# Layer 0's last head in written order, with the first half of its output projection in pieces among it

## The chip, the cores and the metric

The kernel runs on one core of a Trainium2 chip. A core has a matrix engine (TensorE, PE in the profile; its weight loads are shown apart as PEld), three engines that work on elements (VectorE = DVE, ScalarE = ACT, GpSimd = POOL), and a queue that issues transfers (SyncE, SP). Each engine works through its own instructions in program order and waits on semaphores for what the others must have done. The metric is the device time of one execution in microseconds (us).

## What is computed

The program is a two-layer encoder over 1024 tokens of width 1024 in float32. Layer 0 mixes tokens by differential attention, layer 1 by latent attention, and each is followed by a gated MLP with a short convolution. The change lies in layer 0's attention, which is:

```python
def diff_attention(h, w_qkv, ..., subln_g, w_o, lambda_init, cos, sin):
    q, k, v = jnp.split(h @ w_qkv, 3, axis=-1)      # 8 heads; q, k: 2 x 64 wide, v: 128 wide
    q, k = rope on the first 16 of 64 columns
    def block(qb, blk):                              # blocks of 128 queries
        sc = einsum('bqhcd,bkhcd->bhcqk', qb, k) * scale
        p = masked_softmax(sc, chunk_mask(blk, s))
        a = p[:, :, 0] - lam * p[:, :, 1]
        return einsum('bhqk,bkhe->bqhe', a, v)
    o = from_blocks(lax.map(block, ...))
    o = rms_norm(o, subln_g) * (1.0 - lambda_init)
    return o.reshape(b, s, D_MODEL) @ w_o            # then x = x + this
```

The body above is shortened to what matters; the mask is causal by chunks of 64 tokens.

## The kernel before

**Products in three parts.** Operands of TensorE's products are split into a high part (a copy to the short format fp32r, by ACT at L127 or DVE) and a low part (the source less the high part, by DVE or POOL, L130). A product is the sum of three matmuls (L119, L120, L121): high by low, high by high, low by high. So a weight costs a cast (`b` below) and a subtraction (`c`) before it can be used.

**Layer 0's attention.** Eight heads, each in four steps p = 0..3 of two 128-query tiles; step number t = 4 x head + p, 0 to 31. A step scores its queries against the keys up to them (L1804/L1805, two components), takes maxima (DVE), exponentials (ACT, L1830), inverts the sums (DVE), scales the first component's probabilities (ACT L147, or POOL L149 for p < 2), subtracts the second component's (DVE, L1843), transposes them on TensorE against an identity (L1851), splits the transposes, and multiplies with the values. The sum is copied by ACT (L1879). After every second step the head's output (128 x 512 tokens) is normalised: two squares on ACT (L1885, L1888), the low part on POOL, a sum of squares on TensorE (a product with ones, L1896/L1897), roots on ACT, a step of Newton on DVE, and the result is stored in DRAM as o_d (L1917). Meanwhile the next head's keys, queries and values are made in units of half a product each (24 + 12 + 12 matmuls, in PSUM bank u, of which there is one), with rotary mixing (DVE swap and cosine L657, POOL L685), and the next head's weights are split.

**What sets the order.** The function `da_steps` issues the parts of all steps. For t < 28, heads 0 to 6, it reads a row of the table `DA_SCORE` (one of four rows, by t % 4), under a manual schedule, which keeps the engines to the written order. A token of a row is a part's name, with `'` for a step earlier and `+` for the next step: S scores, M maxima, E exponentials, I inverse, C scale, X mix, T transposes, H and L the high and low split of them, A product with the values, O copy, Q squares, F sum of squares, R roots, N Newton; U and V are the step's one or two projection units (`0` and `1` the half-products, `s` and `m` swap and cosine, `p` and `a` POOL's two rotary instructions, `k*` and `q*` the key and query splits, `c t h l` a value's copy, turn and split); Wh and Wl are the high and low part of the next head's weight (Wl on POOL). For t >= 28, head 7, the manual schedule is closed: the parts are issued in an order that depends only on `DA_WHOLE`, and the scheduler that places all the rest of the program places them by its own priorities, so that it may mix head 7 with what stands around it.

**What stands around it.** The output projection w_o comes in eight tiles of 128 rows, one for each head. `prefetcher` loads its tiles 0 to 3 (`step`, called in each of head 7's four `prepare` calls), splits them into the places s0 to s7 as those come free (tile 1's and 3's low part on DVE, the others' on POOL), and loads tiles 4 to 7 into u10 to u13 after head 7. Then `project_first` multiplies the outputs of heads 0 to 3 with w_o's tiles 0 to 3: for each of eight token tiles (in the order 0, 4, 1, 5, 2, 6, 3, 7) it loads the tile of o (L729) into a ring, splits it into two 512-wide pieces of s12, makes two products of 12 matmuls, and adds them to x (into bank u and in two additions for the first four, into one big bank S and in one for the others). After that `project_rest` does the same with the outputs of heads 4 to 7: its first token tile needs the o_d that the last steps of head 7 store.

Of the kernel before, what the change touches and what calls it, by code (L numbers as in the profile page):

```python
# [11 lines left out]
F32R = mybir.dt.float32r  # L12
# [44 lines left out]
class Trunk:  # L57
# [223 lines left out]
    def steps(self, attend, units, prepare, n, apart=False):  # L281
# [3 lines left out]
        for t in range(n + 2):  # L285
# [25 lines left out]
            if t >= 2:  # L311
# [11 lines left out]
    DA_WHOLE = ("S0 M0 M0a M0b E0a E0b I0 C0 X0 S1 M1 M1a M1b E1a E1b I1 C1 X1 Wh Wl "  # L323
                "T0 H0 L0 T1 H1 L1 T2 H2 L2 A0 T3 H3 L3 A1 A2 A3 O Q1 Q2 Q3 F R1 R2 R3 N1 N2 N3").split()

    def da_steps(self, attend, units, prepare, n):
# [3 lines left out]
        region = ExitStack()  # L330
        region.enter_context(self.tc.manual_schedule(engines={E.PE, E.DVE, E.Activation, E.Pool}))
        steps, last = [], 28
        for t in range(-1, n + 2):
            while len(steps) < min(n, t + 2 if t + 1 < last else t + 1):
                x = len(steps)
                steps.append(attend(x))
                steps[x].parts.update(prepare(x))
                us = units(x)
                if x < last:
                    for x, u in zip("UV", us):  # L340
                        steps[-1].parts.update({x + name: f for name, f in u.items()})
            if t >= n:
                us = []
            if t == last:
                region.close()
            if t == 99:
                region.enter_context(self.tc.high_priority())
            for name in self.DA_SCORE[t % 4].split():
                step = t - name.count("'") + name.count("+")
                if 0 <= step < min(n, last):  # L350
                    steps[step](name.strip("+'"))
            if t < last:
                continue
            now = steps[t] if t < n else None
            old = steps[t - 1] if t > last and t <= n else None
            older = steps[t - 2] if t - 2 >= last else None
            if now:
                now("Wh", "Wl", "S0", "M0", "M0a", "M0b", "E0a", "E0b")
            for u in us:
                u.pop("0")()  # L360
            if old:
                old(*self.DA_WHOLE[: self.DA_WHOLE.index("A1")])
            if now:
                now("I0", "C0", "X0", "S1", "M1", "M1a", "M1b", "E1a", "E1b")
# [1891 lines left out]
```

## Time and profile before

| what | us |
|---|---|
| median of three runs (lowest, highest) | 2424.54 (2423.31, 2424.95) |
| the profiled execution | 2427.72 |
| its span (first to last instruction) | 2425.9 |

The profiled execution is one of its own, and about 3 us longer than the median. Its TensorE clock was granted at 0.993 of full speed in the mean.

How to read the rows below: `L1851` is line 1851 of the kernel printed above. `b<-ident,u` says that an instruction writes a tile b and reads tiles ident and u, with numbers left out: tiles u, s and h are places in SBUF of 128 x 1024, 128 x 2048 and 128 x 512 elements, tiles b and S banks in PSUM (and the projection products' bank is also called u). In a timeline a row has start, length, engine, line and operation, shapes, how many instructions were put together, and in brackets how long the engine had been idle before and what ended that. The stretch in question runs from 423.6 us (head 7's first step) to about 540 us (the second half of the output projection); steps of head 0 lie from about 45 us.

### The profile page before, as it was taken

What the parts mean: (1) busy time and instruction counts of PE and PEld (TensorE: products, weight loads), DVE (VectorE), ACT (ScalarE), POOL (GpSimd) and SP (SyncE); (2) the same over time, 40 slices, a digit from 0 to 9 for tenths busy, and PEclk for the clock granted to TensorE, in tenths of its full rate; (3) what the DMA queues carried; (4) which work ended last, traced back from release to release, by engine and by line L of the source; (5) the groups of instructions that cost most, each with busy time, mean ns of one, the idle gap of its engine ahead of it and who ended that gap; (6) DMA issues with size and microseconds to landing.
All of it is one profiled execution on the core that took longest, in us unless ns stands there. A gap on an engine that the chain in (4) does not pass through costs nothing.

```text
span 2425.9 us, 32597 instructions
## 1 busy us (share of the span) xinstructions
PE 2355.7 (97%) x11936; PEld 1999.6 (82%) x11936; DVE 1960.6 (81%) x3175; ACT 1290.5 (53%) x2366; POOL 623.5 (26%) x489
## 2 busy tenths in 40 slices
PE   7999999989999999999999999999989999999998
PEld 7888888778888888878899789988878888887886
DVE  6888888847888888899964788887488888888997
ACT  5677767645444444444445777776344444444444
POOL 4555555424100000000041666664330000000001
PEclk9999999999999999999999999999999999999999
DMA  4011111332222222553221210124322222227502
GB/s 153 31 44 36 35 49 53 105 92 98 94 83 79 87 79 87 189 178 128 76 100 46 77 40 29 49 62 135 92 87 87 78 88 86 79 87 277 172 2 78
DMA packets 95792, 213.91 MB, mean 88 GB/s; under 512 B 8720, under 2 KB 33936, under 8 KB 95632
## 3 DMA queue, kind: packets, MB, share of 16 engines
q1 hardware_dynamic: 86448, 184.04, 23.3%
q10 hardware_dynamic: 9184, 27.79, 3.1%
q8 instruction: 94, 1.54, 0.3%
q14 instruction: 66, 0.54, 0.1%
HBM read 159.37 MB, written 52.43 MB: 87 GB/s over the span
## 4 chain that ended last, share of the span: by engine, by line
PE 82%; DVE 7%; DMA 4%; ACT 3%; POOL 2%; issue 2%; SPq 0%; POOLq 0%; DVEq 0%; ACTq 0%
PE S L119 13%; PE S L121 13%; PE S L120 13%; PE b L119 8%; PE b L120 8%; PE b L121 8%; PE u L119 3%; PE u L121 3%; PE u L120 3%; PE b L252 2%; DVE s L130 2%; PE u L1961 1%; PE u L1960 1%; PE S L1804 1%; PE S L1805 1%
## 5 line engine op out<-in xcount | busy, mean ns | idle before, releaser
L167 POOL TENSOR_TENSOR st<-st,mhalf 128x1 f32<-128x1 f32 x56 | 37.2, 665 | 1308.7 <-DVE st L164 1300.2
L119 PE MATMUL S<-s,u 128*128 128x512 f32 (+1 forms) x768 | 290.3, 378 | 9.4 <-DVE s L130 3.9
L127 ACT CAST u<-h 128x512 fp32r<-128x512 f32 (+2 forms) x242 | 145.8, 619 | 280.9 <-DVE h L988 279.8
L121 PE MATMUL S<-s,u 128*128 128x512 f32 (+1 forms) x768 | 289.3, 377 | 0.1
L120 PE MATMUL S<-s,u 128*128 128x512 f32 (+1 forms) x768 | 289.1, 376 | 0.0
L119 PE MATMUL b<-s,u 128*128 128x512 f32 x588 | 230.8, 392 | 1.8 <-DVE u L130 1.3
L121 PE MATMUL b<-s,u 128*128 128x512 f32 x588 | 229.0, 390 | 0.0
L120 PE MATMUL b<-s,u 128*128 128x512 f32 x588 | 229.0, 389 | 0.0
L1045 DVE SCALAR_TENSOR_TENSOR u<-u,conv,u 128x1023 f32<-128x1023 f32 (+1 forms) x176 | 226.0, 1284 | 1.4 <-ACT u L1041 1.4
L149 POOL TENSOR_TENSOR u<-u,st 128x384 f32<-128x384 f32 (+7 forms) x160 | 172.1, 1084 | 174.8 <-DVE st L1946 104.9
L127 ACT CAST s<-u 128x512 fp32r<-128x512 f32 (+3 forms) x230 | 144.9, 665 | 112.3 <-PE u L121 35.5
L119 PE MATMUL u<-s,s 128*128 128x512 f32 (+1 forms) x440 | 177.2, 403 | 4.0 <-DVE h L657 2.8
L119 PEld LDWEIGHTS S<-s,u 128*128 128x128 f32 x768 | 145.1, 189 | 37.4 <-DVE s L130 4.5
L120 PE MATMUL u<-s,s 128*128 128x512 f32 (+1 forms) x440 | 172.4, 392 | 0.0
L121 PE MATMUL u<-s,s 128*128 128x512 f32 (+1 forms) x440 | 172.4, 392 | 0.0
L130 DVE TENSOR_TENSOR u<-b,u 128x512 fp32r<-128x512 f32 (+1 forms) x256 | 158.7, 631 | 15.5 <-ACT u L127 13.1
L127 ACT CAST u<-b 128x512 fp32r<-128x512 f32 (+1 forms) x256 | 134.7, 546 | 68.6 <-PE b L1851 36.3
L121 PEld LDWEIGHTS S<-s,u 128*128 128x128 f32 x768 | 145.0, 189 | 26.7 <-DVE u L130 0.5
L120 PEld LDWEIGHTS S<-s,u 128*128 128x128 f32 x768 | 145.1, 189 | 26.2
L130 DVE TENSOR_TENSOR s<-u,s 128x512 fp32r<-128x512 f32 (+2 forms) x210 | 151.1, 753 | 14.5 <-ACT s L127 14.1
L1048 ACT ACTIVATE u<-u 128x1024 f32<-128x1024 f32 x44 | 46.7, 1062 | 187.8 <-DVE u L1045 187.7
L130 DVE TENSOR_TENSOR u<-h,u 128x512 fp32r<-128x512 f32 x164 | 112.7, 687 | 32.9 <-ACT u L127 31.8
(280 smaller groups left out, 6570.1 us busy)
## 6 DMA issues: line engine op xcount, KB each, us to landing
u<-in_ffn_up SPq DMA_DIRECT2D x88, 512.0 KB, 4.1
g_d<-u ACTq DMA_DIRECT2D x44, 512.0 KB, 2.6
u<-in_ffn_down SPq DMA_DIRECT2D x66, 256.0 KB, 4.6
u<-g_d SPq DMA_DIRECT2D x62, 256.0 KB, 4.2
s<-in_da_wqkv SPq DMA_DIRECT2D x23, 512.0 KB, 3.6
x_d<-u SPq DMA_DIRECT2D x16, 512.0 KB, 2.9
s<-x_d SPq DMA_DIRECT2D x8, 1024.0 KB, 11.3
u<-o_d SPq DMA_DIRECT2D x24, 256.0 KB, 3.1
```

Of the source, the lines that this page charges most:

```text
L119: mm(out, lh, rl, start=first, stop=False, skip_group_check=onto)
L120: mm(out, lh, rh, start=False, stop=False, skip_group_check=onto)
L121: mm(out, ll, rh, start=False, stop=last, skip_group_check=onto)
L127: self.nc.scalar.copy(out, src)
L130: (eng or self.nc.vector).tensor_sub(out, src, hi.bitcast(F32))
L149: self.nc.gpsimd.tensor_mul(x, x, s.to_broadcast(list(x.shape)))
L167: nc.gpsimd.tensor_tensor(r, s, self.mhalf, ALU.pow)
L252: self.nc.tensor.transpose(ps[:, j * P : (j + 1) * P], probs[t][:, k : k + P], self.ident)
L1045: nc.vector.scalar_tensor_tensor(t[half][:, back:], u[half][:, : S - back], w, t[half][:, back:], ALU.mult, ALU.add)
L1048: nc.scalar.activation(t[0], t[0], AF.Silu)
L1804: nc.tensor.matmul(sc[c][:, b : b + m], ql[c][:, qs], kt[:, c, :m], start=True, stop=False)
L1805: nc.tensor.matmul(sc[c][:, b : b + m], qh[:, c, qs], kt[:, c, :m], start=False, stop=True)
```

## The change

It adds no operation and drops none: every engine issues as many instructions as before. It does four things.

1. `DA_END`: seven written rows for t = 28 to 34, which take the place of the automatic order for head 7 and its last steps. The manual schedule now stays open to the end.
2. The first half of the output projection becomes tokens in these rows (`project_tokens`): `d` `b` `c` load a weight tile of w_o and make its high and low part (0 to 3; for 4 to 7 one `f` loads, then `b` and `c`), `g` `h` `l` load an o tile and make its high and low part, `Y` and `Z` are its two products, `y` and `z` its additions. The low parts c0 and c2 are POOL's, as before; c1, c3 to c7 DVE's.
3. The split tiles of o go into two places from the rings of keys (R.k) and values (R.v), which hold old keys and values by then, and no longer into s12, which holds the rotary table.
4. Row 1 of the table is replaced at t = 1 alone by `DA_SECOND`: the same row, with `Wl` behind `Ua` and no longer ahead of `Q1''`. At t = 1 there is no step two before it, so there the tokens with `''` do nothing.

```diff
+    DA_SECOND = "S0 I1' Vc' Ukd' H2'' M0 L2'' A1'' C0' X0' H3'' E0b L3'' U0 A2'' E0a Wh Vt' N3'''' A3'' O'' Wl' Q2'' C1' I0 X1' U1 C0 S1 X0 Us Vh' Q1'' T0' H0' Q3'' Up F'' Um M1 Ua Wl R1'' Vl' E1b V0 E1a L0' I1 A0' Uqa R2'' R3'' Uqd Uqe Uqb C1 X1 N1'' Uqc V1 T1 T0 Uqf H0"
...
+    DA_END = (
+        "O'' d0 Up X1' S1 S0 V0 R2''' Ua R3''' M1 d1 b0 b1 M0 c0 T0' V1 E1b N1''' T2' H0' L0' E1a c1 Uka +S1 d2 Vc E0a N2''' b2 Ukb E0b N3''' T1' +U0 T3' H2' H1' +M1 I1 +U1 I0 c2 +E1b +E1a L2' L1' d3 +Us A0' +Um C1 C0 H3'",
+        "S0 M0 A1'' Up Ukc' b3 E0a L3'' Ua A2'' X0' A3'' Uqa Ukd' Uqc I1 O'' X1' Q1'' Q2'' Q3'' Uqb Uqd T0' H0' Uqf F'' E0b L0' Uqe g0 c3",
+        "S0 h0 M0a I0' l0 C1' C0' R1''' E0a R2''' M0b g1 A0'' Y0 E0b X1' X0' S1 R3''' h1 g2 T0' N1''' O'' y0 M1b N2''' Vt'' H0' T1' E1b Z0 M1a Vh'' E1a L0' z0 H1' l1 Vl'' L1'",
+        "S0 I1' A0'' h2 C1' I0' A1'' Y1 C0' O'' M0a X1' X0' y1 g3 T0' Q1'' M0b E0a T2' H0' N3'''' T1' H1' E0b L0' I0 l2 C0 Z1 Q2'' L1' z1 H2' h3",
+        "S1' M1b' E1b' Y2 M1a' g4 Q3''' A0'' L2'' y2 E1a' A1'' F''' I1' Z2 C1' X0' R1''' R2''' l3 X1' R3''' T0' g5 z2 N1''' A2'' Y3 H0' O'' h4 L0' y3 T1' l4",
+        "A0'' T2'' H2'' H1'' Z3 L1'' A1'' T3'' N2'''' L2'' H3'' Y4 A2'' h5 L3'' N3'''' g6 A3'' O'' Q1'' l5 z3 Q2'' Z4 g7 f h6 Q3'' Y5 z4 F'' R1'' R2'' l6 Z5",
+        "b4 h7 Y6 R3''' b5 l7 z5 c5 b6 N1''' b7 Y7 c4 Z6 Z7 N2''' N3''' c6 z6 c7 z7",
+    )
...
+    def da_steps(self, attend, units, prepare, n, extra):
...
-        steps, last = [], 28
...
-            while len(steps) < min(n, t + 2 if t + 1 < last else t + 1):
...
-            if t == last:
-                region.close()
...
+        steps, first = [], n - 4
+        with self.tc.manual_schedule(engines={E.PE, E.DVE, E.Activation, E.Pool}):
+            for t in range(-1, first + len(self.DA_END)):
...
+                row = self.DA_SECOND if t == 1 else self.DA_SCORE[t % 4] if t < first else self.DA_END[t - first]
+                for name in row.split():
...
+                    if name in extra:
+                        extra.pop(name)()
+                    elif 0 <= step < n:
+                        steps[step](name)
...
-            if h + 1 == DA_HEADS:
-                prefetch()
...
-            if h + 1 == DA_HEADS:
-                todo = [[(h, 1, 1)], [(h, 0, 1)], [(h, 2, 1)], []][p]
...
-        self.da_steps(lambda t: DaStep(self, R, *divmod(t, 4), heads, o_d), units, prepare, 4 * DA_HEADS)
+        self.da_steps(lambda t: DaStep(self, R, *divmod(t, 4), heads, o_d), units, prepare, 4 * DA_HEADS, project(R.k, R.v))
...
+    def project_tokens(self, w_o, W, places, later, o_d, x_src, X, at, os):
...
+        def low(i):
+            self.lo(W[i][1], raws.pop(i), W[i][0], nc.vector if i % 2 or i >= half else nc.gpsimd)
...
+        def split(n):
...
+            if n < 2:
+                halves.append(os[n]([P, 2, 512], F32R))
+            st.oh, st.ol = (halves[n % 2][:, part].rearrange("p (k s) -> p k s", s=P) for part in range(2))
+            self.hi(st.oh, st.o)
...
+        def product(n, b):
...
+            if n < 4:
+                y = st.y = self.bank("u")
...
+                if b == 0:
+                    st.y = self.big()
+                y = st.y[:, b : b + 512]
+            for k in range(half):
+                self.mm3(y, st.oh[:, k, :], st.ol[:, k, :], W[k][0][:, b : b + 512], W[k][1][:, b : b + 512], k == 0, k == half - 1)
...
+            if n < 4:
...
+            put(f"l{n}", lambda st: self.lo(st.ol, st.o, st.oh, nc.gpsimd), st)
...
+            if n < 4:
...
-        step, finish, rest = prefetcher(a["da_w_o"], W, slots(*range(8)), units(10, 11, 12, 13))
-        k.diff_attention(o_d[0], step)
-        finish()
...
-        X = k.project_first(W, o_d[0], k.ring(*k.cut("s12", 512)), a["x"], at, 2, rest)
+        X = [None] * NT
+        project = lambda *os: k.project_tokens(a["da_w_o"], W, slots(*range(8)), units(10, 11, 12, 13), o_d[0], a["x"], X, at, os)
+        k.diff_attention(o_d[0], project)
```

Head 7's second value unit also moves from step t = 30 to step t = 28, as in the other heads.

TensorE issues the same matmuls in the same order outside a stretch of 480 in the middle, from head 7's first step to the second half of the projection. How the order moves is shown at three places. In the rows below a tile's name carries its numbers: `s_859_4580` is a tile in a place of kind s, the same numbers mean the same tile within one program but not from one program to the other. Line numbers of the changed file are 54 higher in the steps' code (L1804 becomes L1858, L1851 L1905, L1896 L1950), L685 becomes L663.

First, ACT in head 6's last step (t = 27), whose probabilities are `u_808` and whose next head's queries are `u_810`; before:

```order
L1830 ACTIVATE u_807_4307,st_806_4306<-S_4292,st_805_4301 128x768
L1830 ACTIVATE u_808_4315,st_806_4306<-S_4291,st_805_4301 128x768
L127 CAST u_810_4336<-h_802_4288 64x512 x2
L127 CAST s_859_4580<-s_54_146 128x1024
L147 ACTIVATE u_808_4315<-u_808_4315,st_806_4306 128x768
L127 CAST u_810_4336<-h_802_4288 64x512
L1879 COPY h_790_4223<-b_4255 128x256
```

and now:

```order
L1884 ACTIVATE u_807_4307,st_806_4306<-S_4292,st_805_4301 128x768
L1884 ACTIVATE u_808_4315,st_806_4306<-S_4291,st_805_4301 128x768
L127 CAST u_810_4336<-h_802_4288 64x512 x2
L147 ACTIVATE u_808_4315<-u_808_4315,st_806_4306 128x768
L127 CAST u_810_4336<-h_802_4288 64x512
L1933 COPY h_790_4223<-b_4255 128x256
```

The cast of w_o's first tile (`s_859`, from the raw tile `s_54`) has left its place ahead of the scaling of the probabilities. In the same place POOL had:

```order
L130 TENSOR_TENSOR h_55_147<-h_802_4288,u_810_4336 64x512
L130 TENSOR_TENSOR s_859_4580<-s_54_146,s_859_4580 128x1024
L130 TENSOR_TENSOR h_823_4403<-h_817_4382,h_816_4380 128x512
L130 TENSOR_TENSOR s_885_4716<-s_54_146,s_885_4716 128x1024
```

and has now:

```order
L130 TENSOR_TENSOR h_55_147<-h_802_4288,u_810_4336 64x512
L130 TENSOR_TENSOR h_823_4403<-h_817_4382,h_816_4380 128x512
L663 TENSOR_TENSOR h_837_4480<-h_837_4480,s_53_145 128x512
L663 TENSOR_TENSOR h_841_4491<-h_841_4491,h_837_4480 128x512
L130 TENSOR_TENSOR s_847_4534<-s_54_146,s_847_4534 128x1024
L130 TENSOR_TENSOR s_860_4587<-s_54_146,s_860_4587 128x1024
L149 TENSOR_TENSOR u_852_4560<-u_852_4560,st_851_4559 128x256
L149 TENSOR_TENSOR u_859_4584<-u_859_4584,st_858_4583 128x128
```

The two long subtractions of w_o's tiles 0 and 2 (`s_859` and `s_885` before, `s_847` and `s_860` now) stand next to each other in row t = 28, behind the next unit's two rotary instructions and ahead of two scalings of probabilities (L149).

Second, TensorE at the sum of squares of step 27, that is head 6's second half; before:

```order
L120 MATMUL u_5050<-s_886_4719,s_953_5030 128x512
L121 MATMUL u_5050<-s_886_4719,s_953_5030 128x512
L1804 MATMUL S_4784<-u_800_4280,h_57_149 128x512
L1805 MATMUL S_4784<-u_800_4280,u_883_4703 128x512
L1804 MATMUL S_4784<-u_858_4571,h_57_149 128x256
L1805 MATMUL S_4784<-u_858_4571,u_883_4703 128x256
L1896 MATMUL b_4621<-h_865_4619,ones 128x512
L1897 MATMUL b_4621<-h_863_4615,ones 128x512
L1851 MATMUL b_4655<-ident,u_850_4521 128x128
L1851 MATMUL b_4655<-ident,u_855_4550 128x128 x2
```

and now, in row t = 29:

```order
L119 MATMUL b_4648<-u_872_4659,u_769_4122 128x128
L120 MATMUL b_4648<-u_872_4659,u_769_4122 128x128
L121 MATMUL b_4648<-u_872_4659,u_769_4122 128x128
L1905 MATMUL b_4713<-ident,u_859_4584 128x128
L1905 MATMUL b_4713<-ident,u_852_4560 128x128 x2
L1950 MATMUL b_4720<-h_881_4709,ones 128x512
L1951 MATMUL b_4720<-h_880_4707,ones 128x512
L1858 MATMUL S_4730<-u_800_4280,h_57_149 128x512
L1859 MATMUL S_4730<-u_800_4280,u_878_4697 128x512
L1858 MATMUL S_4731<-u_800_4280,h_58_150 128x512
```

Before, the sum stood behind a product of the output projection (`u_5050`) and scores of step 30; now it follows the last product with the values (`b_4648`) after three transposes, and the first scores of step 30 stand behind it.

Third, TensorE at the last sum of squares, that of step 31; before (`S_5269` is the first half's last product, `S_5310` the second half's first token tile):

```order
L121 MATMUL S_5269<-s_886_4719,s_953_5030 128x512
L119 MATMUL S_5310<-s_957_5064,h_978_5302 128x512
L120 MATMUL S_5310<-s_957_5064,h_978_5302 128x512
L1896 MATMUL b_5010<-h_945_5008,ones 128x512
L1897 MATMUL b_5010<-h_944_5006,ones 128x512
L121 MATMUL S_5310<-s_957_5064,h_979_5303 128x512
L119 MATMUL S_5310<-s_963_5132,h_978_5302 128x512
L120 MATMUL S_5310<-s_963_5132,h_978_5302 128x512
```

and now:

```order
L120 MATMUL S_5189<-s_875_4677,u_899_4796 128x512
L121 MATMUL S_5189<-s_875_4677,u_899_4796 128x512
L1950 MATMUL b_5203<-h_964_5187,ones 128x512
L1951 MATMUL b_5203<-h_959_5162,ones 128x512
L119 MATMUL S_5189<-s_847_4534,u_899_4796 128x512
L120 MATMUL S_5189<-s_847_4534,u_899_4796 128x512
L121 MATMUL S_5189<-s_847_4534,u_899_4796 128x512
```

Before, the last sum stood within the second half's first token tile; now five of the first half's products (60 matmuls, of token tiles 5 to 7) come behind it, and then the second half.

99 lines of the change are left out of this document (54 added, 45 removed).

## The prediction

> **What bounds the kernel now.** I read the page's busy shares first, then the list of who waited for whom on TensorE, then the timeline around its longest waits. The first fence is from the page and the list of TensorE's waits (engine, line, what it waited for: total us, times, longest).
>
> ```profile
> span 2425.9 us, 32597 instructions
> PE 2355.7 (97%) x11936; PEld 1999.6 (82%) x11936; DVE 1960.6 (81%) x3175; ACT 1290.5 (53%) x2366; POOL 623.5 (26%) x489
> PE S L119 <- ACT h L127: 5.9, 1, 5.9
> PE b L1851 <- DVE u L1843: 5.3, 2, 3.9
> PE u L119 <- DVE h L657: 2.8, 3, 2.0
> PE S L121 <- POOL s L130: 1.0, 1, 1.0
> ```
>
> TensorE is busy for 97% and idle for 70.2 us. The change adds and drops no matmul: it can only take idle time of TensorE away, or bring new. All four waits quoted lie, for the most part, in the stretch that is reordered. Each gets a look.
>
> The first is at the start of head 7. Rows: start, length, engine, line, operation, and in brackets the idle time before it.
>
> ```profile
> 422.32 1.05 ACT L127 CAST s<-s 128x1024 fp32r<-128x1024 f32 x1
> 423.27 0.94 ACT L147 ACTIVATE u<-u,st 128x768 f32<-128x768 f32 x1
> 424.24 5.41 DVE L1843 SCALAR_TENSOR_TENSOR u<-u,st,u 128x768 f32<-128x768 f32 x1 [1.45 <-ACT u L147]
> 425.28 2.34 POOL L130 TENSOR_TENSOR s<-s,s 128x1024 fp32r<-128x1024 f32 x1
> 429.71 2.40 PE L1851 MATMUL b<-ident,u 128*128 128x128 f32 x10 [3.93 <-DVE u L1843]
> 432.33 0.63 PE L120 MATMUL u<-s,s 128*128 128x512 f32 x1
> 432.76 0.63 PE L121 MATMUL u<-s,s 128*128 128x512 f32 x1
> 434.46 0.51 PE L119 MATMUL u<-s,s 128*128 128x512 f32 x1
> 438.24 0.39 PE L120 MATMUL u<-s,s 128*128 128x512 f32 x1
> 438.46 0.39 PE L121 MATMUL u<-s,s 128*128 128x512 f32 x1
> 367.46 1.47 DVE L1843 SCALAR_TENSOR_TENSOR u<-u,st,u 128x768 f32<-128x768 f32 x1 [0.50 <-ACT u L147]
> ```
>
> The last row is the same instruction one head earlier: 1.47 us, against 5.41 here. What differs is the first and fourth row: the scheduler put the first output weight's split (ACT 1.05, POOL 2.34) among head 6's last steps. TensorE stood for 3.93 us, and then matmuls began 0.43 us apart instead of 0.22, until 434.46: half of 4.75, so 2.4 more. Together **6.3**.
>
> The next, with the split of the second weight on DVE ahead of it (2.31 us), costs 1.39 + 0.35 = **1.7**; L121's wait for POOL at a projection product costs **1.0** (first fence).
>
> ```profile
> 441.88 2.31 DVE L130 TENSOR_TENSOR s<-s,s 128x1024 fp32r<-128x1024 f32 x1
> 451.74 0.88 PE L1851 MATMUL b<-ident,u 128*128 128x128 f32 x6 [1.39 <-DVE u L1843]
> 452.96 0.50 PE L119 MATMUL u<-s,s 128*128 128x512 f32 x1 [0.35 <-DVE h L657]
> ```
>
> The longest is at the attention's end. The last row is of the windows view: length, busy PE, PEld, DVE, ACT, POOL, granted clock, DMA share, GB/s.
>
> ```profile
> 528.70 0.39 PE L1897 MATMUL b<-h,ones 128*128 128x512 f32 x1
> 532.75 0.75 DVE L1916 SCALAR_TENSOR_TENSOR h<-h,g_sub,h 128x512 f32<-128x512 f32 x1
> 535.82 0.39 SPq L729 DMA_DIRECT2D u<-o_d  x1
> 539.32 0.62 ACT L127 CAST h<-u 128x512 fp32r<-128x512 f32 x1 [2.78 <-DMA u<-o_d]
> 540.00 0.80 PE L119 MATMUL S<-s,h 128*128 128x512 f32 x1 [5.89 <-ACT h L127]
> 540.00:550.00 10.00, 9.87 (x39) 7.67 (x40) 3.10 (x3) 2.30 (x4) 4.30 (x4) 0.80 0.20 57
> ```
>
> From the sum of squares (L1897) the head's output is normalised, stored, read back and split before token tile 4 can be multiplied: 540.00 - 528.70 = 11.3 us, for which TensorE had too little other work. 5.89 idle, and a clock of 0.80 over the next 10 us, 2.0: **7.9**.
>
> The last one is in head 0.
>
> ```profile
> 60.05 3.73 DVE L1843 SCALAR_TENSOR_TENSOR u<-u,st 128x256 f32<-128x256 f32 x2
> 60.81 2.56 POOL L130 TENSOR_TENSOR s<-s,s 128x1024 fp32r<-128x1024 f32 x1
> 64.33 0.67 DVE L657 TENSOR_TENSOR h<-u,s 128x512 f32<-128x512 f32 x1
> 65.06 0.50 PE L119 MATMUL u<-s,s 128*128 128x512 f32 x1 [1.96 <-DVE h L657]
> 66.09 0.63 PE L120 MATMUL u<-s,s 128*128 128x512 f32 x1
> 69.08 0.58 PE L121 MATMUL u<-s,s 128*128 128x512 f32 x1
> ```
>
> While POOL makes a weight's low part, two DVE products take 3.73 us; L657, which frees the one-buffer bank u, is late; TensorE idles 1.96 and then runs slowly from 66.09 to about 69.5, 1.7 more: **3.7**.
>
> **The change part by part.** *Step 1's own row* moves that POOL instruction behind the two rotary products, so the DVE products run beside a short POOL instruction and bank u is free in time: +3.7. Price: POOL's scaling of the step's probabilities then queues behind those 2.56 us. Bounds 0 and 1.96 (the wait it replaces); a projection half-product stands between, so I take 0.5.
>
> *The weights' splits* leave head 6's rows, which then are the rows of earlier heads: +6.3. Splits and scores in written order also end the waits at 451.74 (+1.7) and at L121 (+1.0). Costed at nothing: the DMAs of weights, x and o_d. The loads sit on SP one or two rows ahead of their casts, and a step's half-products cover them; a late one would hold ACT, whose next casts feed TensorE, for a DMA's 539.32 - 535.82 = 3.5 us at worst.
>
> *The end.* After the last L1897 pair, five projection pieces now follow, 60 matmuls, then token tile 0 of the second half, 24. At 0.22 to 0.23 us that is 19 us of cover for a chain of 11.3. The chain gets longer: a weight's and an o tile's cast between its ACT instructions (1.05 + 0.62) and two weights' low parts between its DVE ones (2.31 each at most): 17.6. So +7.9, and nothing lost unless 1.4 us or more are added.
>
> Gross: 3.7 + 6.3 + 1.7 + 1.0 + 7.9 = **20.6**.
>
> *What is new* is in row t = 29 and the two after it. Behind product A3 of step 27 TensorE finds only one group of three transposes before the sum of squares. That sum waits for copy, two squares and POOL's rounding, which the trace has for the last step:
>
> ```profile
> 522.05 0.36 ACT L1879 COPY h<-b 128x256 f32<-128x256 f32 x1
> 522.45 0.63 ACT L1885 ACTIVATE h<-h 128x512 f32<-128x512 f32 x1
> 522.99 0.62 ACT L1888 ACTIVATE h<-h 128x512 fp32r<-128x512 f32 x1
> 523.68 1.30 POOL L130 TENSOR_TENSOR h<-h,h 128x512 fp32r<-128x512 f32 x1 [7.48 <-ACT h L1888]
> ```
>
> 524.98 - 522.05 = 2.93, less three transposes (0.88 for six: 0.44), plus about 0.1 for handing over: **2.6** of idle. Queued behind the sum are the next scores; their second half waits for ACT's query casts, which stand five instructions behind the squares.
>
> ```profile
> 453.00:500.00 47.00, 46.95 (x256) 40.34 (x257) 38.96 (x75) 33.71 (x71) 17.70 (x15) 1.00 0.28 86
> 367.80:423.60 55.80, 55.05 (x301) 47.14 (x301) 47.65 (x82) 40.36 (x80) 30.39 (x22) 1.00 0.17 57
> ```
>
> Five at 33.71/71 = 0.475 are 2.4; POOL's rounding (1.3) and the sum (0.46) cover the rest, which leaves **0.6**. Then density. A normal head (second row) has 82 DVE records for 301 matmuls, 0.27 each, at 47.65/55.8 = 85% busy. Rows 29 to 31 hold 46 for 139 by the order, 0.33: the same rate of matmuls would need DVE for 104%. At the mean matmul of the first row (46.95/256 = 0.183) these rows are 25.5 us; TensorE loses 1.0 if DVE works without a pause, and 25.5 x (1.04/0.85 - 1) = 5.7 if it again reaches 85%. DVE catches up while TensorE waits for the sum, so I take **2.3**, nearer the low end. New idle: 2.6 + 0.6 + 2.3 = **5.5**, bounds 3.2 and 8.9.
>
> The clock: 1.96 us of idle at 65.06 was followed by slow matmuls, 1.39 + 0.35 at 451.74 was not. Here two waits of some 1.3 us stand either side of three transposes: between these; I take **1.3** of 0 to 2.4. The Trainium skill (TensorE: Matmul & The Clock Gate, section HAM oscillation) says gaps of TensorE above about 3.4 us bring the slow clock; by that this term is 0 and the time 1.3 lower. The row at 65.06, 1.96 and slow after it, doesn't agree, so the row decides.
>
> Sum: 20.6 - 0.5 - 5.5 - 1.3 = **13.3** off the profiled execution's 2427.72 (span 2425.9 and 1.8 around it): 2414.4. That execution is 3.2 above the runs' median of 2424.54, so **2411**.
>
> **The rivals.**
> 1. *Only the provable wait comes.* New idle 3.2, no slow clock: 20.6 - 3.2 = 17.4, 2407. For it: head 7 before ran DVE for 38.96 of 47 us (83%) beside a full TensorE. Against: 104%.
> 2. *DVE bounds the rows.* 8.9 + 2.4 + 1.0 new: 9.3 or less gained, 2415; with one late load (3.5) 2419. For it the two ratios above; against, the filler from row 30 on.
> 3. *The end's wait stays.* SP issues in order, and the load of tile 0 stands behind two weight loads that wait for the last step's buffers; ACT has tile 0's cast ahead of the root. If that costs more than the 1.4 of margin plus 5.89, the 7.9 are not gained: 5.4, 2419. Against: the buffers come free with the last transposes, over 8 us (36 matmuls) ahead.
> 4. *Slower: DVE held by POOL.* The row at 424.24 shows a DVE product with both inputs in SBUF stretched by 5.41 - 1.47 = 3.9 beside POOL. Rows 28 to 31 issue some 18 such instructions beside two long and a dozen short POOL ones. Five such hits with TensorE straight behind make 13.3 into -6.2: 2431; it decides from the fifth. For it: row 28 has both long POOL splits; against: four half-products of 12 matmuls stand in that row. The Trainium skill (SBUF, section SBUF: two separate sides) says the later of the two waits for the other's whole instruction; the 5.41 agrees with more than one such wait. By one wait on 2.34 a hit it would need eight.
>
> **How the numbers follow.** Forecast 52%, own range 2408 to 2415. Rival 1: 13%; rival 2: 16%; rival 3: 9%; rival 4: 10%. Range 2403 to 2423: it takes in rivals 1 to 3 and three hits of rival 4 (2411 + 3 x 3.9), and leaves its fourth and further hits, and more gain than 4 beyond rival 1, outside. A measurement of this kernel can't tell less than about 0.2% (4.8 us) from nothing: faster means below 2419.7. Forecast, rival 1, and most of 2 and 3 lie there: 0.80; same, the rest of 2 and 3: 0.10; slower, rival 4: 0.10.
>
> **What would show it.** Right: L1843 of 128x768 near 424 takes about 1.5; no wait of L119 for ACT h L127 above 1 us after the last sum of squares; no wait of u L119 for L657 near 63; a new wait of TensorE for POOL's rounding ahead of a sum of squares, 1.2 to 2.6 us, some 20 us into head 7; the first projection's pieces end some 14 us earlier against 534. Wrong: waits of bank u on DVE at several pieces (rival 2 or 4), or tile 4 again waiting over 3 us (rival 3).

## The result and the profile after

| kernel | median, us | the kernel before beside it | ratio (95% interval) |
|---|---|---|---|
| changed | 2412.62 (2411.2 to 2414.68, 4 runs) | 2424.57 | 0.9952 (0.9935 to 0.997) |
| changed, measured again | 2412.19 (2412.15 to 2412.6, 5 runs) | 2427.30 | 0.9935 (0.9921 to 0.9949) |

The change makes the kernel 12 to 15 us faster; 2411 was predicted. The kernel before differs by 2.7 us between the two sets of runs, so kernels of different sets are compared by ratio, and closer by their traces: the times at which both start the same 512-wide matmuls, as the median difference over 12 us of matmuls. Changed less before: -0.2 us at 45 us, -2.5 at 80, -2.6 at 415, -9.1 at 440, -14.9 at 560, -15.0 at 1340, -13.9 at 2390. So the gain is complete 20 us behind the stretch that was reordered; the spans differ by 2425.9 - 2412.9 = 13.0, since single executions drift by 1 to 2 us in the long rest.

The head of the changed kernel's page:

```profile
span 2412.9 us, 32605 instructions
PE 2353.4 (98%) x11936; PEld 2000.5 (83%) x11936; DVE 1953.6 (81%) x3175; ACT 1290.7 (53%) x2366; POOL 621.2 (26%) x489
```

Its list of TensorE's waits (total, times, longest):

```profile
PE b L1950 <- POOL h L130: 3.1, 7, 0.5
PE b L1905 <- DVE u L1897: 2.3, 2, 1.6
PE u L119 <- DVE h L635: 0.6, 2, 0.5
```

The waits of 5.9 for ACT, 3.9 for the mix, 2.0 for bank u and 1.0 for POOL are gone. Two shorter ones for the mix (1.6 and 0.7) have come.

The timeline at the end of head 6, where 3.9 us were lost:

```profile
419.76 0.94 ACT L147 ACTIVATE u<-u,st 128x768 f32<-128x768 f32 x1
420.73 1.47 DVE L1897 SCALAR_TENSOR_TENSOR u<-u,st,u 128x768 f32<-128x768 f32 x1 [0.50 <-ACT u L147]
422.96 1.36 PE L1905 MATMUL b<-ident,u 128*128 128x128 f32 x11
```

The mix takes 1.47 us and is done 0.76 ahead of the transposes. Next, the attention's end:

```profile
507.59 0.39 PE L1951 MATMUL b<-h,ones 128*128 128x512 f32 x1
517.04 0.33 SPq L1971 DMA_DIRECT2D o_d<-h  x1
521.81 0.62 ACT L127 CAST h<-u 128x512 fp32r<-128x512 f32 x1 [7.27 <-DMA u<-o_d]
526.89 0.39 PE L119 MATMUL S<-s,h 128*128 128x512 f32 x1
```

Its windows view for the first ten microseconds of tile 4:

```profile
526.80:536.80 10.00, 9.72 (x48) 7.87 (x47) 5.24 (x7) 4.51 (x8) 3.68 (x4) 1.00 0.45 146
```

From the last sum of squares to the split of token tile 4 it takes 522.43 - 507.98 = 14.5 us, longer than before; TensorE reaches the tile 4.5 us later still, without a wait, and the next 10 us run at full clock (0.80 before).

Row t = 29, the only place in the stretch that still loses time:

```profile
453.31 0.37 ACT L1933 COPY h<-b 128x256 f32<-128x256 f32 x1
453.92 1.07 DVE L1897 SCALAR_TENSOR_TENSOR u<-u,st 128x256 f32<-128x256 f32 x1
454.94 1.27 POOL L130 TENSOR_TENSOR h<-h,h 128x512 fp32r<-128x512 f32 x1 [0.24 <-ACT h L1942]
452.36 0.39 PE L119 MATMUL b<-u,u 128*128 128x256 f32 x1 [0.35 <-DVE u L130]
455.04 0.69 PE L1905 MATMUL b<-ident,u 128*128 128x128 f32 x2 [1.64 <-DVE u L1897]
456.26 0.80 PE L1950 MATMUL b<-h,ones 128*128 128x512 f32 x1 [0.54 <-POOL h L130]
```

The windows view there:

```profile
451.50:456.20 4.70, 2.24 (x14) 1.44 (x12) 3.40 (x7) 4.60 (x10) 3.73 (x3) 0.86 0.44 164
456.20:461.80 5.60, 5.54 (x18) 4.87 (x19) 4.07 (x9) 4.08 (x9) 4.33 (x5) 0.51 0.25 73
```

Copy to POOL's rounding takes 456.21 - 453.31 = 2.90 us, as predicted (2.93), and TensorE idles 0.35 + 1.64 + 0.54 = 2.53. The larger part is named after DVE: the same gap holds the transposes, which wait for a mix that comes 1.6 us late. Then the clock is granted at 0.51 for 5.6 us: 5.6 x 0.49 = 2.7 us more. (The slow stretch begins some 1.3 us earlier, but there TensorE has only two transposes to do, and the idle time is counted already.)

And the row of t = 1:

```profile
63.08 0.50 PE L119 MATMUL u<-s,s 128*128 128x512 f32 x1 [0.17 <-DVE h L635]
65.14 2.42 POOL L130 TENSOR_TENSOR s<-s,s 128x1024 fp32r<-128x1024 f32 x1
68.58 1.74 DVE L1897 SCALAR_TENSOR_TENSOR u<-u,st 128x512 f32<-128x512 f32 x1 [2.19 <-POOL u L149]
70.38 0.88 PE L1905 MATMUL b<-ident,u 128*128 128x128 f32 x6 [0.69 <-DVE u L1897]
```

Bank u comes free nearly in time (a wait of 0.17 for 1.96); the scaling waits behind the moved POOL instruction, the mix behind that, and TensorE 0.69 for the mix. Up to the matmul ahead of that wait the row has gained 3.4 us, behind it 2.3.

### The profile page after: what moved, and what is told of

The parts are those of the page before. It is cut to its first block, busy times and chain, and to the rows that moved or that the text cites. A ratio compares the mean times of both kernels' runs of the same rounds, so it can differ in the third digit from the quotient of the medians.

```text
span 2412.9 us, 32605 instructions
## 1 busy us (share of the span) xinstructions
PE 2353.4 (98%) x11936; PEld 2000.5 (83%) x11936; DVE 1953.6 (81%) x3175; ACT 1290.7 (53%) x2366; POOL 621.2 (26%) x489
## 4 chain that ended last, share of the span: by engine, by line
PE 85%; DVE 6%; ACT 3%; DMA 3%; POOL 1%; issue 1%; SPq 0%; POOLq 0%; DVEq 0%; ACTq 0%
PE S L119 13%; PE S L121 13%; PE S L120 13%; PE b L119 8%; PE b L120 8%; PE b L121 8%; PE u L119 4%; PE u L121 4%; PE u L120 4%; PE b L252 2%; PE u L2015 1%; DVE s L130 1%; PE u L2014 1%; PE S L1859 1%; PE S L1858 1%
## 5 line engine op out<-in xcount | busy, mean ns | idle before, releaser
L119 PE MATMUL S<-s,u 128*128 128x512 f32 (+1 forms) x800 | 304.0, 380 | 6.8 <-DVE u L1136 3.7
L121 PE MATMUL S<-s,u 128*128 128x512 f32 (+1 forms) x800 | 303.0, 379 | 0.1
L120 PE MATMUL S<-s,u 128*128 128x512 f32 (+1 forms) x800 | 302.7, 378 | 0.0
L149 POOL TENSOR_TENSOR u<-u,st 128x512 f32<-128x512 f32 (+7 forms) x160 | 172.0, 1084 | 168.5 <-DVE st L2000 105.0
L119 PEld LDWEIGHTS S<-s,u 128*128 128x128 f32 x800 | 152.1, 190 | 35.6 <-ACT s L127 4.0
L130 DVE TENSOR_TENSOR u<-b,u 128x512 fp32r<-128x512 f32 (+1 forms) x256 | 158.7, 631 | 20.8 <-ACT u L127 18.2
L121 PEld LDWEIGHTS S<-s,u 128*128 128x128 f32 x800 | 152.0, 190 | 28.1 <-DVE u L130 0.5
L120 PEld LDWEIGHTS S<-s,u 128*128 128x128 f32 x800 | 152.1, 190 | 27.3
L119 PE MATMUL u<-s,s 128*128 128x512 f32 (+1 forms) x408 | 163.4, 401 | 1.9 <-DVE s L130 0.9
L130 DVE TENSOR_TENSOR s<-u,s 128x512 fp32r<-128x512 f32 (+2 forms) x210 | 151.1, 754 | 9.7 <-ACT s L127 9.4
L121 PE MATMUL u<-s,s 128*128 128x512 f32 (+1 forms) x408 | 158.8, 389 | 0.0
L120 PE MATMUL u<-s,s 128*128 128x512 f32 (+1 forms) x408 | 158.6, 389 | 0.0
L130 DVE TENSOR_TENSOR u<-h,u 128x512 fp32r<-128x512 f32 x164 | 112.8, 688 | 32.5 <-ACT u L127 31.5
```

What stands on the lines that cost most here:

```text
L119: mm(out, lh, rl, start=first, stop=False, skip_group_check=onto)
L120: mm(out, lh, rh, start=False, stop=False, skip_group_check=onto)
L121: mm(out, ll, rh, start=False, stop=last, skip_group_check=onto)
L130: (eng or self.nc.vector).tensor_sub(out, src, hi.bitcast(F32))
L149: self.nc.gpsimd.tensor_mul(x, x, s.to_broadcast(list(x.shape)))
```

## The experiments

Each was timed in five rounds beside the kernel before. Pieces of a row stand in the diffs, not whole rows.

| kernel | median, us | before | ratio (95% interval) |
|---|---|---|---|
| row1_alone | 2438.70 | 2427.11 | 1.0042 (1.0029 to 1.0055) |
| cast_early | 2427.45 | 2427.11 | 0.9996 (0.9988 to 1.0005) |
| split_early | 2429.78 | 2427.11 | 1.0012 (1.0003 to 1.0021) |
| value_late | 2412.57 | 2427.11 | 0.9938 (0.9926 to 0.9951) |
| row1_undone | 2414.59 | 2426.47 | 0.9953 (0.994 to 0.9965) |
| split_early_2 | 2419.97 | 2426.47 | 0.9967 (0.9957 to 0.9978) |
| cover_48 | 2419.86 | 2426.47 | 0.9971 (0.9961 to 0.9982) |
| split_s12 | 2412.35 | 2426.47 | 0.9941 (0.9927 to 0.9955) |
| row29_filled | 2410.57 | 2427.30 | 0.993 (0.9917 to 0.9943) |
| row29_wl | 2411.26 | 2427.30 | 0.9929 (0.9915 to 0.9943) |
| cover_48_b | 2419.87 | 2427.30 | 0.997 (0.9959 to 0.9981) |

**The row of t = 1 alone.** The kernel before, with `DA_SECOND`:

```diff
-            for name in self.DA_SCORE[t % 4].split():
+            for name in (self.DA_SECOND if t == 1 else self.DA_SCORE[t % 4]).split():
```

> The kernel before, with only the row of t = 1 replaced (Wl behind Ua); head 7 stays in the automatic order. Theory (the two rows' gains add, and the one at t = 1 is a POOL matter): the wait of 1.96 us of L119 for L657 near 65 us and the slow matmuls behind it go (-3.6), a wait of the transposes for the mix takes 0.7 to 0.9 of it back; -2.7 us, so about 2422 against 2424.6. The trace then differs from that of the kernel before up to about 75 us and is shifted as a whole behind it. Rival (the gain at t = 1 is eaten by the next wait that stands anyway): within 0.5 us of the kernel before, at 70 to 100 us in the trace already.

Against the kernel before it stood at +0.1 us at 45, -2.2 at 80, -3.5 at 1340: near the theory's gain of 2.7 at t = 1. But at 1700 us it stood at +6.8. Some 10 us are lost in layer 1, 1,300 us behind the edit. TensorE's waits from 1360 to 1650 us, first of this kernel and then of the kernel before:

```profile
PE b L252 <- DVE u L130: 4.8, 9, 0.9
PE S L119 <- ACT u L1942: 2.9, 3, 2.2
PE b L252 <- DVE S L1940: 1.2, 1, 1.2
```

```profile
PE b L119 <- DVE u L130: 1.3, 3, 0.6
PE b L252 <- DVE u L130: 1.2, 2, 0.8
```

The order of the instructions differs there: from TensorE's 6,584th matmul to its 8,444th the scheduler, which places layer 1 by itself, has chosen another one. Neither theory held for the time. cast_early and split_early got the same other order and lost 11.4 and 11.1 us in the same stretch (1340 to 1700 us); the changed kernel has the order of the kernel before. value_late has another order in part of the stretch too (6,584th to 7,085th matmul) and stands 1.5 us worse against the changed kernel at 1700 us than at 1340, so its ratio is not of the edit alone. All the other kernels keep layer 1's order. Which orders go with which edit was not settled.

**One weight's split back among head 6's rows.** In t = 26 (both), and in t = 27 (split_early alone). The load `d0` goes to the head of row t = 26, and what has moved is taken out of `DA_END`:

```diff
-Uqa Uqd C1 Uqf
+Uqa Uqd b0 C1 Uqf
-Uqc' L1' Q3''
+Uqc' c0 L1' Q3''
```

> The changed kernel with the load and the high part (d0, b0) of w_o's first tile back in step 26's row, on ACT ahead of the scaling of step 26's second probabilities, as the automatic order had it; its low part stays where the change put it. Theory (most of the 3.9 us wait came from POOL's long subtraction beside the DVE mix, not from the cast): the mix of 768 columns starts 0.9 us later and takes 1.5 us; TensorE waits 0.2 us or less; the time is that of the changed kernel within 1 us. Rival (the cast ahead of the scaling makes the wait): TensorE waits 1 us or more ahead of the eleven transposes near 423 us, and 2 to 6 us are lost.

> As the kernel with the early cast, and the low part (c0, POOL) also back, behind the query's low parts in the row of t = 27. Theory (POOL's long subtraction stretches the DVE mix): the mix takes over 4 us, TensorE waits 3 to 4 us ahead of the transposes and is slow for some 4 us behind, and the time is 5 to 6.5 us above the changed kernel, about 2418. Rival (the automatic order lost the time in another way, such as by a different order of TensorE's own matmuls): the mix takes about 1.5 us and the time is within 1 us of the changed kernel.

> As the kernel before it (t = 1 as before), and w_o's first tile split early again: high part on ACT in step 26's row, low part on POOL in the row of t = 27; unlike in the first try, layer 1's order is that of the kernel before. Theory (POOL's subtraction beside the mix stretches it, TensorE waits 3.9 us and is slow behind): 4 to 5.5 us slower than the kernel with only the row of t = 1 undone, a ratio of about 0.998. Rival (the first try's loss was layer 1's order, not this): within 1 us of that kernel.

The timeline of cast_early, and then of split_early_2 (which keeps layer 1's order):

```profile
422.55 1.88 DVE L1899 SCALAR_TENSOR_TENSOR u<-u,st,u 128x768 f32<-128x768 f32 x1 [1.46 <-ACT u L147]
424.49 1.31 PE L1907 MATMUL b<-ident,u 128*128 128x128 f32 x10 [0.40 <-DVE u L1899]
```

```profile
424.06 5.42 DVE L1897 SCALAR_TENSOR_TENSOR u<-u,st,u 128x768 f32<-128x768 f32 x1 [1.45 <-ACT u L147]
422.24 2.88 POOL L130 TENSOR_TENSOR h<-h,u 64x512 fp32r<-64x512 f32 x2 [2.45 <-issue]
425.09 2.35 POOL L130 TENSOR_TENSOR s<-s,s 128x1024 fp32r<-128x1024 f32 x1
427.41 1.25 POOL L130 TENSOR_TENSOR h<-h,h 128x512 fp32r<-128x512 f32 x1
429.54 1.31 PE L1905 MATMUL b<-ident,u 128*128 128x128 f32 x10 [3.94 <-DVE u L1897]
```

The cast alone makes TensorE wait 0.40 (0.2 or less was expected) and costs 0.85 us against the changed kernel (+0.86 at 415 us, +1.71 at 440); with the POOL instruction the mix takes 5.42 us (5.41 before) and TensorE waits 3.94 (3.93). At 440 us split_early_2 stands 5.8 us behind the kernel with only t = 1 undone, at 475 to 2390 us 4.2 to 4.8; by ratio (0.9967 against 0.9953) 3.4. The first split_early had shown the same 5.8 at 440. That 1.2 us of it are gone by 475 us has nothing to do with the split: in row 29 TensorE's slow stretch happened to be 3.41 us long in split_early_2 and 6.83 in row1_undone. So the theory holds: POOL's subtraction beside the DVE mix is nearly all of the price, and the cast 0.85 of the 5.8.

**The row of t = 1 undone in the changed kernel**, with layer 1's order kept:

```diff
-                row = self.DA_SECOND if t == 1 else self.DA_SCORE[t % 4] if t < first else self.DA_END[t - first]
+                row = self.DA_SCORE[t % 4] if t < first else self.DA_END[t - first]
```

> The changed kernel with the row of t = 1 as before; all else of the change stays, and layer 1's instructions stand in the order of the kernel before. Theory (the row of t = 1 is worth what its own stretch shows, 2.6 to 2.8 us by about 75 us): 2.7 us slower than the changed kernel, about 2415 where the kernel before takes 2424.6, a ratio of 0.996. Rival (what is gained at t = 1 is lost again at a later wait): within 0.7 us of the changed kernel, a ratio of 0.995.

-0.1 us against the changed kernel at 45 us, +2.3 at 80, +2.6 at 1700: close to the theory's 2.6 to 2.8, and the third trace that shows 2.3 to 2.4 for this row. The ratio (0.9953) lies within the changed kernel's first interval, and its own overlaps the second, so the time alone couldn't tell it.

**The place of the split tiles.** They go into two halves of s12, the rotary table's place:

```diff
-                halves.append(os[n]([P, 2, 512], F32R))
+                halves.append(os(n))
...
+                place.extend(k.cut("s12"))
+            return k.at(place[n], [P, 2, 512], F32R)
```

> The changed kernel with the split tiles of o in s12, the rotary table's place, as before, and not in the places of old keys and values. Theory (the table's last reader, POOL's rotary product in the row of t = 29, is done before the first split begins in the next row, so the place changes nothing): within 1 us of the changed kernel. Rival (the first split has to wait there, and ACT with it): ACT waits at the first split, scores or roots come late, 2 us or more are lost.

```profile
451.59 1.28 POOL L663 TENSOR_TENSOR h<-h,h 128x512 f32<-128x512 f32 x1
458.17 0.62 ACT L127 CAST s<-s 128x512 fp32r<-128x512 f32 x1
```

The last rotary instructions end at 452.87, the first split starts 5.3 us later. From 80 to 560 us it stands 0.2 us behind the changed kernel, as it does at 45 us, ahead of the edit: this part of the change has no time of its own.

**Less cover at the end.** The last sum of squares behind Z6, and then once more with z6 ahead of it:

```diff
-Y5 z4 F'' R1'' R2'' l6 Z5
-b4 h7 Y6 R3''' b5 l7 z5 c5 b6 N1''' b7 Y7 c4 Z6 Z7 N2''' N3''' c6 z6 c7 z7
+Y5 z4 l6 Z5
+b4 h7 Y6 b5 l7 z5 c5 Y7 Z6 F''' R1''' R2''' R3''' b6 N1''' b7 c4 Z7 N2''' N3''' c6 z6 c7 z7
```

> The changed kernel with the last sum of squares 48 matmuls later (behind Z6 and no longer behind Y5), so that 36 matmuls are left to cover its chain and not 84. Theory (the chain from that sum to the split of token tile 4 is 14.4 us, as the trace of the changed kernel shows it, with 4.5 us to spare): 48 matmuls are 10.9 us, so TensorE waits some 6 us ahead of tile 4 and is slow behind it, 6.5 to 8.5 us in all. Rival (most of the 14.4 us is the weights' splits that stand among it on ACT and DVE, done by then in the later place, so that the bare 11.3 us are left): it waits some 3 us, 3.3 to 5 us in all.

> As the kernel with the last sum of squares 48 matmuls later, but with the first half's addition z6 ahead of that sum's chain on DVE. In the first try the 5 us wait stood ahead of token tile 0 of the second half: its bank is freed by z6, and z6 stood on DVE behind the Newton steps, which wait for the sum; the tile of o itself was split 11.1 us behind the sum, not 14.4. Theory now (the bare chain is some 11.3 us, and what the 14.4 had more are weights' splits that fill spare time): no wait ahead of tile 0, 2 to 3 us ahead of tile 4, 3.5 to 5.5 us in all over the changed kernel. Rival (the chain is 14.4 us as such): a wait of 5 to 6 us ahead of tile 4.

cover_48's timeline, and cover_48_b's waits from 500 to 546 us:

```profile
518.56 0.39 PE L1951 MATMUL b<-h,ones 128*128 128x512 f32 x1
525.42 1.22 DVE L776 TENSOR_TENSOR s<-s,S 128x1024 f32<-128x1024 f32 x1
526.69 0.80 PE L119 MATMUL S<-s,h 128*128 128x512 f32 x1 [4.99 <-DVE s L776]
529.21 0.62 ACT L127 CAST h<-u 128x512 fp32r<-128x512 f32 x1 [6.26 <-DMA u<-o_d]
```

```profile
PE b L855 <- DVE u L958: 2.9, 1, 2.9
PE S L119 <- DVE s L130: 2.4, 3, 1.4
PE S L121 <- POOL h L130: 0.5, 1, 0.5
```

The cost came (0.9971 and 0.997; between 500 and 560 us 7.9 and 8.2 us), but neither time where either theory had put it. That cover_48's 7.9 lies in its theory's range of 6.5 to 8.5 is luck: the wait is for a bank, not for the chain. The chain itself is 529.83 - 518.95 = 10.9 us here, near the 10.9 of before, so the 14.5 of the changed kernel hold weights' splits in spare time, as the rival said. But DVE works in order: in cover_48 the addition that frees a bank stood behind the Newton steps, and with that mended the second half's weights (s, L130) and then its normalisation (L958) were late. The cover hides a chain and the weights' splits, both on DVE.

**Work for the gap in row 29.** The query unit ahead of the value unit, and the value's second half-product behind the last product:

```diff
-S0 V0 R2''' Ua R3''' M1 d1 b0 b1 M0 c0 T0' V1 E1b
+S0 +U0 R2''' Ua R3''' M1 d1 b0 b1 M0 c0 T0' +U1 E1b
-Q3'' Uqb Uqd T0' H0' Uqf F''
+Q3'' V1' Uqb Uqd T0' H0' Uqf Vc' F''
```

> The changed kernel with head 7's query unit ahead of its value unit, and the value unit's second half-product (12 matmuls) in the row of t = 29 between the last product of step 27 and the transposes, so that TensorE has 2.7 us of work while copy, squares and POOL's rounding of the sum of squares run. Theory (what is left of the row's loss is that one chain, 2.9 us with no work beside it, and the slow matmuls behind the wait): 2.5 us of idle and 2.8 to 3.4 of slow matmuls go, so 4 to 6 us faster than the changed kernel, about 2407. Rival (DVE bounds the rows, and the wait only moves): the time stays within 1.5 us of the changed kernel, with waits for DVE at several places of the rows 29 and 30.

row29_filled moves besides L2' ahead of +M1, b2 behind H1', the query's Up and Ua into row 28, c2 behind C0, and E0b and X1' ahead of the casts:

> The changed kernel with the value unit's second half-product behind the last product of step 27, as in value_late, and with what gave half of that gain back mended: the split of the transposes (L2') earlier on DVE, so that the bank for step 27's product comes free; the cast that waits for a weight's load (b2) behind the casts of the transposes on ACT; the query's rotary product earlier, the long POOL split behind the scalings; the second exponentials ahead of the casts. Theory (the 5.9 us that rows 29 to 30 lose between 451 and 462 us in the changed kernel are the sum's chain, 2.5 of idle, and the slow matmuls behind it, and no engine bounds these rows): 4.5 to 6 us faster than the changed kernel, a ratio of about 0.993. Rival (DVE bounds the rows after all, and every wait only moves): at most 2.5 us faster, like value_late, with waits for DVE elsewhere between 440 and 470 us.

The waits of value_late and then of row29_filled from 440 to 465 us, and row29_filled's windows there:

```profile
PE b L119 <- DVE u L130: 1.9, 2, 1.5
PE S L1858 <- ACT u L1884: 0.8, 1, 0.8
```

```profile
PE b L119 <- DVE u L130: 2.9, 3, 1.1
PE b L1950 <- POOL h L130: 0.4, 1, 0.4
```

```profile
440.00:456.00 16.00, 13.07 (x73) 10.68 (x72) 14.57 (x23) 10.71 (x28) 10.27 (x8) 1.00 0.48 164
```

The same window of value_late, and then of the changed kernel:

```profile
440.00:456.00 16.00, 14.13 (x80) 11.78 (x79) 12.51 (x25) 11.53 (x28) 9.63 (x9) 1.00 0.49 165
440.00:456.00 16.00, 13.74 (x77) 11.37 (x75) 12.70 (x24) 11.60 (x27) 8.92 (x8) 0.97 0.67 231
```

The wait for the mix and the slow clock go, and DVE's splits of the transposes are late in their place. Between 415 and 475 us value_late gains 1.8 us on the changed kernel and row29_filled 0.9; on one chip row29_filled has 0.993 against 0.9935, within the intervals. Even the 1.8 flatter the edit: cover_48, whose rows are the changed kernel's up to there, gains 1.1 us in this stretch merely because its slow stretch in row 29 lasts 3.41 us and not 6.83. So the rival's signs came: the waits moved to DVE. That DVE bounds the rows by its whole share is not shown: it works without a pause from 440.5 us up to the split that TensorE waits for (447.66, 1.28 long), but over the window it is busy for 12.51 of 16.00 us, less than in the changed kernel. The 14.57 of row29_filled is in part POOL's doing. In row29_filled the query's rotary products also came beside DVE instructions with two inputs in SBUF:

```profile
444.37 1.43 DVE L1968 SCALAR_TENSOR_TENSOR h<-h,h 128x512 f32<-128x512 f32 x1
445.83 1.68 DVE L644 SCALAR_TENSOR_TENSOR u<-h,u 64x512 fp32r<-64x512 f32 x1
```

In the changed kernel these two take 0.69 and 0.68 (at 441.84 and 442.56): 1.7 us of DVE lost to waiting for POOL.

**The weight's low part still later at t = 1** (behind Uqf, in the kernel with the filled row):

```diff
-M1 Ua Wl R1''
-V1 T1 T0 Uqf H0
+M1 Ua R1''
+V1 T1 T0 Uqf Wl H0
```

> The kernel with the filled row 29, and at t = 1 the weight's low part on POOL still later, behind the query's low parts. Theory (the 0.69 us wait for the mix that the change left near 70 us comes from that POOL instruction ahead of the scaling): 0.5 to 0.9 us less than with the filled row 29 alone, seen in the trace by about 80 us, since a comparison of times can hardly tell it. Rival (the next half-product then waits for the weight's low part): no gain, or up to 1 us lost there.

```profile
PE u L121 <- POOL s L130: 0.6, 1, 0.6
```

The wait for the mix (0.7) goes and the next half-product waits 0.6 for the low part: 0.2 us by 80 us. The rival's wait. No version here beats the changed kernel by more than its interval.

**The changed kernel once more:**

> The changed kernel itself, for a comparison on the same chip as the three that follow, and a closer interval. Theory (nothing but the measurement differs): a ratio to the kernel before of 0.994 to 0.9965, some 12 us. Rival (the first measurement was off): a ratio outside of that.

0.9935 (0.9921 to 0.9949): the ratio lies just below the range expected, by its letter the rival's sign. But the intervals of both sets overlap, and the trace agrees with the first to 0.3 us from 45 to 560 us.

## Why the prediction was right

| term | predicted | measured | by |
|---|---|---|---|
| t = 1, net | 3.7 - 0.5 = 3.2 | 3.4 - 1.0, 2.3 to 2.4 | changed, row1_alone, row1_undone |
| splits leave head 6's rows | 6.3 | 6.5; put back 5.8 | changed; split_early_2 |
| waits at 451 and 507 us | 2.7 | gone | list of waits |
| the end | 7.9 | its wait and its slow clock gone | changed |
| new idle in rows 28 to 31 | 5.5 | 2.5 | the three waits in row 29 |
| new slow clock | 1.3 | 2.7 | windows of row 29 |
| sum | 13.3 | 14.7 at 560 us, 13.0 over the span | traces |

**t = 1.** The mechanism was right: the DVE products beside a short POOL instruction, bank u in time. The gain ahead of the price was 3.4, not 3.7 (a wait of 0.17 stays), and the price 1.0 (a wait of 0.69 and what restarts), not 0.5: the mix waits for the scaling behind the POOL instruction, within the bounds 0 to 1.96.

**Head 6's end.** Right in size. Its place was named imprecisely: the mix at 424 us is of step 26, in the last row of head 6 (t = 27), not of head 7's first step. "What differs is the first and fourth row" left two causes together; the runs separate them, and POOL's is nearly all. The 1.47 us that the prediction took for the undisturbed mix already holds a wait for POOL; undisturbed it takes 1.01 (last section), so that POOL's part of the 5.41 is 4.4 and not 3.9.

**The end.** The cover worked as worked out (14.5 of about 19 us, the margin 4.5 and not 1.4). Shown by the trace; the runs with less cover cost some 8 us but by DVE's queue, so that they confirm the cover's worth and not the chain alone.

**Row 29.** The 2.6 of idle were 2.53, on the chain that was named (2.90 for 2.93), though mostly recorded as a wait for the mix, which ends in the same gap. The 0.6 for the scores fell away. The step that was mis-sized is the density, 2.3, with its sentence "DVE catches up while TensorE waits for the sum": DVE did, more than was allowed for, and 0.35 was left. That the term is real is seen in value_late: with the gap filled, waits of 1.9 for DVE come. The clock was mis-sized the other way, 2.7 against 1.3 and a bound of 2.4, and its size is partly chance: in cover_48 the same gaps bring a slow stretch half as long. The two errors cancel in part: 5.2 against 6.8 in all.

**The sum.** The terms as measured add up to 2.35 + 6.5 + 2.7 + 7.9 - 2.5 - 2.7 = 14.2 of the 14.7 at 560 us; the last 0.5 is not put down to anything. That the forecast came so near owes something to luck: it had the idle time 3.0 too high, the slow clock 1.4 too low and t = 1 0.9 too good.

**The signs.** L1843's 1.47, no wait for ACT at the end and 0.17 at 63 us came. The new wait for POOL's rounding came at 456 us, some 30 us into head 7 and not 20, and under POOL's name only 0.54 us of it. "The first projection's pieces end some 14 us earlier" did not: the second half's tile 0 starts 6.6 us earlier (521.45 for 528.01), and only tile 4 is 13.1 earlier, since before the wait stood between them.

**The rivals.** 1 and 2 differ by DVE's pauses and by the clock. The idle time lies at rival 1's end (2.5 for 3.2), the clock beyond rival 2's (2.7 for 2.4), and the time between the two. Their sums have slips, which the forecast doesn't share: rival 1's 17.4 leaves out the 0.5 of t = 1, and its 3.2 the 1.0 that the working gives as the least for density; rival 2's 9.3 leaves out the 0.5 and its own 1.0, with which it would be 7.8. Rival 3's load came in time. Rival 4's hits, DVE held by POOL, didn't come in the changed kernel's rows, but did in split_early_2 and row29_filled. None of the rivals had the largest danger that the runs showed: that layer 1's automatic order changes with an edit in layer 0.

## What to carry to other kernels

In a kernel that a scheduler partly orders, compare the order far behind an edit too, and judge a local edit by the same instructions' times in the two traces: 2.3 us gained at 65 us became 11.6 us lost in the time. A long POOL subtraction should not stand beside a DVE instruction with two inputs in SBUF that TensorE waits for, least of all in a row of POOL instructions without a pause. A gap of TensorE that an engine used to catch up in is not free to fill: look first at what that engine does in the gap.

## What the runs showed of the hardware

A DVE instruction with two inputs in SBUF can be held up by several POOL instructions in a row. Where no POOL instruction runs beside it, the mix of 768 columns takes 1.01 us, as here in the kernel before:

```profile
484.94 1.01 DVE L1843 SCALAR_TENSOR_TENSOR u<-u,st,u 128x768 f32<-128x768 f32 x1
```

In heads 0 to 6 a POOL instruction ends 0.66 us after the mix has started, and it takes 1.47. In cast_early that end comes 1.06 after the start, and it takes 1.88. In split_early_2 three POOL instructions without a pause end 4.60 after the start, and it takes 5.42 (5.41 in the kernel before). Each time the mix ends 0.81 to 0.82 us behind POOL's last end. The Trainium skill (SBUF — State Buffer, section SBUF: two separate sides) has the later of the two wait for the other's whole instruction; the three lengths agree with that. They add that POOL can keep the mix out: in split_early_2 the second and the third POOL instruction begin 0.03 to 0.04 us ahead of the recorded end of the one before, while beside the 1.47 the next one begins 0.07 behind that end, and the mix comes in. That this pause decides is read from these two patterns alone.

TensorE's clock fell behind shorter gaps than the Trainium skill states (TensorE: Matmul & The Clock Gate, section HAM oscillation: above about 3.4 us). One gap of 1.96 us at 65 us (kernel before) and 1.64 + 0.54 around two transposes (changed) were followed by slow matmuls; 1.52 alone (value_late) and 1.09, 0.99 and 0.84 some 3 us apart (row29_filled, granted clock 1.00) were not. The length of a gap alone doesn't decide it: a gap of 2.60 us in the changed kernel (at 1768.7 us) was followed by a granted clock of 0.51, and one of 2.59 in the kernel before (at 1784.4) by 1.00. Away from the kernel's ends, each slow stretch in these traces is one at half clock of 3.41 or 6.83 us, and which one comes varies behind the same gaps: in row 29 it is 6.83 in five traces and 3.41 in four. At 1346 us one execution of the changed kernel has such a stretch, and the other, with the same gaps, has none. What decides was not tried.
